# Two output projections in seven block products instead of eight, in a one-core decoder trunk

## The chip, the cores and the metric

The kernel runs on one core of one Trainium2 chip. A core has several engines that run side by side, each with its own queue of instructions in order: TensorE (PE in the profile, with its weight loads as PEld), VectorE (DVE), ScalarE (ACT), GpSimd (POOL) and SyncE (SP), which here only issues transfers. TensorE multiplies a stationary tile of 128x128 by a moving tile of up to 512 columns and adds the result up in PSUM, a memory of eight banks of 128 x 512 fp32; everything else lies in SBUF, which has 128 partitions. The metric is the device time of one execution in microseconds (us); lower is better. An execution is compared with others of the same kernel by the median.

## The reference

Two layers over 1024 rows of 1024 columns in fp32. Each layer runs 12 mixer heads (layer 0: latent attention over all earlier rows; layer 1: attention in a window of 128 rows) and 4 heads over a memory of 256 rows; their outputs of 64 columns each are put side by side, go through one output projection `w_o` of 1024x1024, and are added to the residual. Then follows an MLP. Cut to what matters:

```python
for i in range(DEPTH):                       # DEPTH = 2
    hn = rmsnorm(x, attn_norm_g[i])
    mix, q_cross = mla_mixer(...) if i % 2 == 0 else swa_mixer(...)   # 12 heads x 64
    cross = memory_cross_attention(q_cross, mem_n, w_mem_kv[i])       # 4 heads x 64
    x = x + jnp.concatenate([mix, cross], axis=-1) @ w_o[i]           # the projection
    x = x + squared_relu_mlp(rmsnorm(x, mlp_norm_g[i]), mlp_w_up[i], mlp_w_down[i])
return rmsnorm(x, final_norm_g)
```

## The kernel before

Every fp32 matmul is made of three matmuls of a faster type. `split` (L96) cuts a tile into a high part (a copy on ScalarE, L99) and a low part (a subtraction on VectorE, L100), and `mm3` (L105) adds hi x hi, hi x lo and lo x hi into one PSUM tile (L108 to L110). A product of 128x128 by 128x512 therefore costs three matmuls of 512 columns and, once for each operand, one split.

The program is written as Python that emits instructions. A scheduler orders them at compile time: an instruction is put where its operands and its buffer are ready, in the order of the program where several are, so a load is often issued long ahead of the place where it is written. On the chip each engine then works off its queue in order. Nearly all transfers are issued from SP's queue; the residual's copies into DRAM (`xd`) go by POOL's queue. Tiles are named by tags, and two tiles with one tag share memory: the later one waits for the last reader of the earlier. `quad` holds the large ones (`q0`, `q1`, `f0`, `f1`, and two of `raw`), the `Mlp` object the rest (`i`, `d`, `g`, `x`, `u`).

The work around the projection in each layer:

- *Attention.* The heads' outputs end in two tiles `o[0]` and `o[1]` of 128 x 4 x 1024, features on partitions: together eight k tiles of 128 features by 1024 rows. In layer 0 a head's output is divided by its softmax sum after the fact. For the last head, 11, this is `LastHead` (L1010): the sums go to DRAM, are spread over 64 partitions by another transfer (L1021), and multiplied in (L1028). Its columns lie in k tile 1 of the second half. One of its two halves of rows (G=1) is done at the end of the attention through the list `tails`, the other (G=0) inside the projection.
- *Output projection*, `wo_phase` (L1207): two halves of 512 columns of `w_o`; in each, eight tiles of 128 rows; in each, eight k tiles x 3 matmuls of 128x512: 384 matmuls a layer into tiles `pswo`. Half 0's weights are loaded and split by `WoHalf` (L620) during the attention into `q0` and `q1`; half 1's during half 0 into `g0` to `g3`. For layer 1, `wo_ahead` (L659) makes half 0's split weights some 130 us ahead into DRAM, from where they are loaded again. Each result is added to the residual on VectorE (L1315 in half 0, L1351 in half 1). In half 1 a row tile is then complete: its mean square and its root (L1194 to L1203), the normalised rows (`norm`, L1270) and their transposition (`xT_`, L1278: eight TensorE transposes, L1286, copies by ScalarE, L1289, and for row tiles 4 to 7 four subtractions on VectorE, L1293 to L1296) follow one row tile behind the matmuls; the last row tile's transposition (`m.last_T`) stands in the MLP's first steps.
- *MLP*, `mlp` (L1380). It is already made of seven block products in place of eight. Its operand is cut into two row halves and two column halves; `X[1]` and `X[2]` are the split blocks of rows 0 to 511, written by `xT_`, while `X[3]` to `X[7]` are splits of differences (`prep_x`, L1450). The weight blocks' sums are made by `sum_w` (L1399; L1407 to L1410 are its four operations). The first two of 16 column groups have their products 1 and 2 ahead of the rest, with weights made by `fill_w` (L1370) during the projection; so the order is (0,1), (0,2), (1,1), (1,2), then the other products of these two groups, and then group 2 with its product (2,1) and so on (`go`, L1542; matmuls at L1468 to L1470, results on VectorE at L1499 to L1532).

PSUM is divided in two ways: in the attention of layer 0 six tiles of one bank and one of two (`new_psum(1)`), elsewhere two tiles of two banks (`ps2`) and four of one (`ps1`). The change back stands after `wo_phase(0, ...)`.

Three other places matter for the change. In layer 0, before the attention, `values_of` (L602, tile `psv`) makes the heads' values in eight steps, then six steps make the keys (`pskn`), and then the queries' weights are loaded and split: `wqn` into the pool `wu`, `wqn2` into a pool `wu2` that is opened there; the queries (`psqn`) read them, beside the rotary part (`q_rope`, VectorE). In layer 1, `wo_ahead` runs during the last four jobs of the input projection in two quarters of `f1`, and `s_qk(0, ...)` then writes `f1`. The tiles that `WoHalf.step` fills are filled during the attention, a step every few units.

## Time and profile before

| | |
|---|---|
| runs of the kernel before | 2116.82, 2120.81, 2121.93 us; median 2120.81 |
| the profiled execution | 2116.59 us, of which the span of the trace is 2114.9; granted TensorE clock 0.998 |
| busy share of the span | PE 98%, PEld 81%, DVE 70%, ACT 54%, POOL 8% |
| output projection, layer 0 | first matmul 446.72, end of the last 539.3 us |
| output projection, layer 1 | first matmul 1394.49, end of the last 1487.4 us |
| first product of group 2 of the MLP, (2,1) | 582.43 in layer 0, 1528.64 in layer 1 |

The page of the profile gives shares over the whole span; they are averages over stages with different limits. A row of the timeline gives an instruction's start, its duration, its engine, line and tiles, and in brackets how long the engine had been idle before it and what released it. Matmuls are pipelined: a row's duration (0.39 us) is longer than the distance to the next row. In the chain of waits, a row is a piece of the path that ended last. Lines are those of the kernel before.

### The profile page before, as it was taken

To read this page: it belongs to the slowest core of one execution; us is meant where nothing else is said; L and a number is where in the kernel's file an instruction comes from. 1 tells how busy PE (TensorE), PEld (TensorE's weight loads), DVE (VectorE), ACT (ScalarE), POOL (GpSimd) and SP (SyncE) were. 2 spreads that over 40 slices of the span, in tenths; PEclk is the share of its full clock that TensorE was granted. 3 is DMA by queue.
4 is the path that set the end of the run, shared out by engine and by line. 5 is a ranking of instruction groups with operands and counts; after the bars stand their busy time and mean duration, and the time that the engine had idled before them with its cause. 6 is when DMAs were issued, how large, how long until landed. Compare 5 with 4: busy or idle time off the path is not lost.

```text
span 2114.9 us, 29110 instructions
## 1 busy us (share of the span) xinstructions
PE 2078.4 (98%) x9928; PEld 1708.0 (81%) x9928; DVE 1470.6 (70%) x2833; ACT 1134.6 (54%) x2444; POOL 159.6 (8%) x224
## 2 busy tenths in 40 slices
PE   7999999999999999999999999999999999999998
PEld 6988777788788878888888878778888878788886
DVE  7555588865977776976657553866976775976565
ACT  5455477776754443444445553976745443444452
POOL 0013100001000000000001241620000000000000
PEclk9999999999999999999999999999999999999999
DMA  7202123342354446944433241242344446844342
GB/s 247 68 1 76 46 65 92 105 143 100 110 170 162 140 136 218 337 159 143 150 119 95 66 146 54 81 137 73 133 146 159 157 139 230 317 151 155 118 122 85
DMA packets 177070, 282.92 MB, mean 134 GB/s; under 512 B 17581, under 2 KB 73370, under 8 KB 176922
## 3 DMA queue, kind: packets, MB, share of 16 engines
q1 hardware_dynamic: 170480, 265.30, 39.2%
q0 software_dynamic: 4016, 13.12, 1.8%
q10 hardware_dynamic: 2426, 2.65, 0.4%
q8 instruction: 78, 1.28, 0.3%
q14 instruction: 70, 0.57, 0.1%
HBM read 187.47 MB, written 81.05 MB: 127 GB/s over the span
## 4 chain that ended last, share of the span: by engine, by line
PE 80%; DVE 7%; DMA 6%; ACT 4%; issue 2%; SPq 0%; POOL 0%; DVEq 0%; ACTq 0%; POOLq 0%
PE psy L1805 5%; PE psy L1803 5%; PE psy L1804 5%; PE psz L1805 4%; PE psz L1803 4%; PE psz L1804 4%; PE pss L930 4%; PE pso L972 4%; PE psu L1468 3%; PE psu L1470 3%; PE psu L1469 3%; DMA mr<-in_mlp_w_up_dram 3%; PE pswo L108 3%; PE pswo L110 3%; PE pswo L109 2%; PE psf L108 2%
## 5 line engine op out<-in xcount | busy, mean ns | idle before, releaser
L1368 ACT ACTIVATE mr<-mr,gcol 128x256 f32<-128x256 f32 (+1 forms) x160 | 67.3, 477 | 81.2 <-DMA mr<-in_mlp_w_up_dram 77.5
L1368 ACT ACTIVATE d<-d,gcol 128x256 f32<-128x256 f32 x128 | 57.7, 499 | 79.0 <-DMA d<-in_mlp_w_up_dram 61.7
L1803 PE MATMUL psy<-g 128*128 128x512 f32 x256 | 99.9, 390 | 0.0
L1804 PE MATMUL psy<-g 128*128 128x512 f32 x256 | 99.6, 389 | 0.0
L1805 PE MATMUL psy<-g 128*128 128x512 f32 x256 | 99.4, 389 | 0.0
L99 ACT ACTIVATE g<-i 128x512 fp32r<-128x512 f32 x79 | 49.6, 628 | 89.1 <-PE psz L1804 46.3
L100 DVE TENSOR_TENSOR g<-i,g 128x512 fp32r<-128x512 f32 x79 | 55.5, 703 | 48.9 <-ACT g L99 48.9
L99 ACT ACTIVATE uh<-i 128x512 fp32r<-128x512 f32 x66 | 41.6, 630 | 86.1 <-PE psy L1804 40.7
L99 ACT ACTIVATE i<-mr 128x512 fp32r<-128x512 f32 x78 | 49.1, 629 | 70.8 <-PE psy L1804 20.6
L951 ACT ACTIVATE p<-pss 128x512 f32<-128x512 f32 x108 | 63.6, 593 | 41.1 <-PE pss L930 41.0
L100 DVE TENSOR_TENSOR pl<-p,ph 128x512 fp32r<-128x512 f32 (+1 forms) x96 | 61.5, 651 | 27.4 <-ACT ph L99 26.9
L805 DVE TENSOR_REDUCE m<-psx 128x1 f32<-128x128 f32 (+5 forms) x96 | 70.1, 747 | 11.0 <-PE psx L801 10.8
L100 DVE TENSOR_TENSOR uh<-i,uh 128x512 fp32r<-128x512 f32 x66 | 45.6, 690 | 44.7 <-ACT uh L99 44.7
L1804 PE MATMUL psz<-g 128*128 128x512 f32 x192 | 74.7, 389 | 0.0
L1805 PE MATMUL psz<-g 128*128 128x512 f32 x192 | 74.7, 389 | 0.0
L1803 PE MATMUL psz<-g 128*128 128x512 f32 x192 | 74.7, 389 | 0.0
L100 DVE TENSOR_TENSOR i<-mr,i 128x512 fp32r<-128x512 f32 x78 | 53.6, 687 | 22.0 <-ACT i L99 21.6
L1684 DVE TENSOR_TENSOR mqf<-mqq,mqf 128x512 f32<-128x512 f32 x64 | 43.1, 686 | 21.9 <-DMA mqq<-in_mlp_w_down_dram 21.7
L99 ACT ACTIVATE ph<-p 128x512 fp32r<-128x512 f32 (+1 forms) x96 | 56.4, 599 | 1.3
L1805 PEld LDWEIGHTS psy<-g 128*128 128x128 f32 x256 | 48.1, 188 | 10.0
L1804 PEld LDWEIGHTS psy<-g 128*128 128x128 f32 x256 | 48.1, 188 | 9.9
L1803 PEld LDWEIGHTS psy<-g 128*128 128x128 f32 x256 | 48.1, 188 | 9.8
(658 smaller groups left out, 6913.4 us busy)
## 6 DMA issues: line engine op xcount, KB each, us to landing
i<-hd SPq DMA_DIRECT2D x154, 256.0 KB
hd<-uh SPq DMA_DIRECT2D x76, 256.0 KB
hd<-ul SPq DMA_DIRECT2D x76, 256.0 KB
mr<-in_mlp_w_up_dram SPq DMA_DIRECT2D x36, 512.0 KB
hd<-x SPq DMA_DIRECT2D x72, 256.0 KB
mr<-hd SPq DMA_DIRECT2D x70, 256.0 KB
d<-in_mlp_w_up_dram SPq DMA_DIRECT2D x32, 512.0 KB
mqq<-in_mlp_w_down_dram SPq DMA_DIRECT2D x32, 512.0 KB
```

The costliest lines, as they stand in the source:

```text
L99: nc.scalar.activation(hi, src, AF.Copy)
L100: nc.vector.tensor_tensor(lo, src, f32(hi), ALU.subtract)
L108: nc.tensor.matmul(ps, ah, bh, start=first and i == 0, stop=False)
L110: nc.tensor.matmul(ps, al, bh, start=False, stop=last and i == n - 1)
L805: nc.vector.reduce_max(m8s[h][:, i : i + 1], ps[:, c], axis=AX, negate=True)
L930: return lambda: nc.tensor.matmul(o, a, b, skip_group_check=True, **kw)
L951: nc.scalar.activation(p, ps, AF.Exp, scale=SC)
L972: mms.append(lambda: nc.tensor.matmul(o, a, b, skip_group_check=True, **kw))
L1368: nc.scalar.activation(w[:, k, :], w[:, k, :], AF.Copy, scale=g_mlp[layer][:, k0 + k : k0 + k + 1])
L1803: nc.tensor.matmul(ps, ah[:, j, :], bh, start=p in (1, 5, 2) and k == 0, stop=False, skip_group_check=True)
L1804: nc.tensor.matmul(ps, ah[:, j, :], bl, start=False, stop=False, skip_group_check=True)
L1805: nc.tensor.matmul(ps, al[:, j, :], bh, start=False, stop=k == NP - 1, skip_group_check=True)
```

## The change

The product of activations and `w_o` is cut into 2x2 blocks: rows 0 to 511 and 512 to 1023, k tiles 0 to 3 and 4 to 7, columns 0 to 511 and 512 to 1023. Seven products of such blocks, each of 4 row tiles x 4 k tiles x 3 matmuls of 128x512, replace the eight. Their operands are the blocks themselves or sums of blocks, and their results are added into the output blocks.

- *Weights.* `wo_sums` makes four sums of weight blocks (for products 5, 7, 6 and 4) in eight pieces of 256 columns, splits them and stores the parts to DRAM; a piece has four loads, four subtractions, four splits and eight stores, and all pieces use the same 128 x 6 x 256 tile. In layer 0 it runs beside `values_of` and the keys, in a pool `wop` that is released before `wu2` is opened; in layer 1 in the quarters of `f1`, in the place of `wo_ahead`, with two steps at a time. `WoRaw` replaces `WoHalf`: during the attention it loads the two raw blocks b11 and b22 into `q0` and splits b11 into `q1`.
- *Projection.* `wo_phase` runs 28 steps: products 1, 5, 6, 3, 2, 7, 4, each with k tiles 0, 2, 3, 1. Activation sums (`sums`) are made on VectorE up to seven steps ahead, the splits (`prep`) up to four. Weight sums come back from DRAM in `prep`. Products 1, 6, 7 and 4 add up in the PSUM tiles `pswy`, products 5, 3 and 2 in `pswz`, and at the end of each product four additions put the tiles into the output blocks. Rows 0 to 511 are complete after product 2 and are normalised in place during product 7; rows 512 to 1023 are complete after product 4, whose matmuls run row tile by row tile. Row tiles 0 to 3 are transposed during product 4, tile 4 after it, and tiles 5 to 7 in the MLP between its first products (`m.late`).
- *Last head.* Both halves of head 11 are divided after the first four preparations of the projection (`last_heads`), where PSUM is divided anew, too.

The diff, cut to its core (lines of context and of the removed `WoHalf`, `wo_ahead` and old `wo_phase`, which are shown above, are left out):

```diff
     def split(src, hi, lo, scale=None):

         if scale is None:
-            nc.scalar.activation(hi, src, AF.Copy)
+            r = nc.scalar.activation(hi, src, AF.Copy)
             nc.vector.tensor_tensor(lo, src, f32(hi), ALU.subtract)
+            return r
...
+    def w_rows(layer, k, cols, dst):
+        if layer == 0 or k > 5:
+            nc.sync.dma_start(out=dst, in_=w_o[layer, k * P : k * P + P, cols])
+            return
...
+    wts = {}
+    def wo_sums(layer, buf):
+        ds = wts[layer] = {p: [dram.tile([P, 4, 512], F32, name=f"wt{layer}_{p}{e}") for e in "hl"] for p in (5, 7, 6, 4)}
+        s = [buf[:, i, :] for i in range(6)]
+        V = nc.vector.tensor_tensor
+        def run():
+            for n in range(8):
+                k, c = divmod(n, 2)
+                cs = [slice(e * 512 + c * 256, e * 512 + c * 256 + 256) for e in range(2)]
+                for i, (kt, e) in enumerate(((k, 0), (k, 1), (k + 4, 1), (k + 4, 0))):
+                    w_rows(layer, kt, cs[e], s[i])
+                yield
+                V(s[0], s[1], s[0], ALU.subtract)
+                V(s[1], s[2], s[1], ALU.subtract)
+                V(s[2], s[2], s[0], ALU.subtract)
+                V(s[3], s[3], s[2], ALU.subtract)
+                for i, p in enumerate((5, 7, 6, 4)):
+                    hi, lo = s[4 + i % 2].bitcast(F32R), s[i].bitcast(F32R)
+                    split(s[i], hi, lo)
+                    for d_, t_ in zip(ds[p], (hi, lo)):
+                        nc.sync.dma_start(out=d_[:, k, c * 256 : c * 256 + 256], in_=f32(t_))
+                    if i % 2:
+                        yield
+        return run()
+    class WoRaw:
+        def __init__(self, layer):
+            self.layer, self.n = layer, 0
+        def step(self):
+            n, k = self.n, self.n % 4
+            self.n += 1
+            if n == 0:
+                self.q = quad_tile("q0", f"wor{self.layer}")
+            if n == 4:
+                self.q1 = quad_tile("q1", f"wob{self.layer}", F32R)
+            if n < 4:
+                w_rows(self.layer, k, slice(0, 512), self.raw(0, k))
+                w_rows(self.layer, k + 4, slice(512, 1024), self.raw(1, k))
+            elif n < 8:
+                split(self.raw(0, k), *self.b1(k))
+        def raw(self, e, k):
+            return self.q[:, k, e * 512 : e * 512 + 512]
+        def b1(self, k):
+            return [self.q1[:, k, e * 512 : e * 512 + 512] for e in range(2)]
+    wop = pool("wop", "right")
+    summing = wo_sums(0, wop.tile([P, 6, 256], F32, name="wos"))
...
         values_of(t)
+        for _ in range(2):
+            next(summing, None)
-    class WoHalf:
...
-    def wo_ahead(buf):
...
+        for _ in range(2):
+            next(summing, None)
         nc.vector.tensor_copy(kn[j][:, 0:512], ps[:, 0:512])
         nc.scalar.activation(kn[j][:, 512:1024], ps[:, 512:1024], AF.Copy)
+    wop.release()
     wu2 = pool("wu2", "right")
     wqn = rows(wpair(wu, 2, 768, "wqn", "a"), 2) + rows(wpair(wu2, 1, 768, "wqn2", "c"), 1)
...
-    wq = WoHalf(0, 0, quad_slots())
+    wq = WoRaw(0)
...
-        if n == len(seq) + LB - 2:
-            tails[0].spread(at.tile([P, 512], F32, tag="p", bufs=4, name="rb11"))
     for _ in muls:
         pass
-    tails[0].mul()
...
-    def wo_phase(layer, wq, o, m):
...
+    def wo_phase(layer, wo, o, m, head=None):
+        ADD, V = ALU.add, nc.vector.tensor_tensor
+        X, xr = {}, {}
+        m.X, m.xr, m.t2, m.fill = X, xr, {}, []
+        steps = [(p, k) for p in (1, 5, 6, 3, 2, 7, 4) for k in (0, 2, 3, 1)]
+        N = len(steps)
+        a1 = [m.t(f"i{2 * j}")[:, 0, :] for j in range(4)]
+        u2 = [m.t(f"i{2 * j + 1}")[:, 0, :] for j in range(4)]
+        a5 = [v_[:, j, :] for v_ in (m.t("d2"), m.t("d3")) for j in range(2)]
+        c21 = []
+        def load(dst, r, c):
+            for j in range(4):
+                nc.sync.dma_start(out=dst[j], in_=m.x_src[r * 512 + j * P : r * 512 + j * P + P, c * 512 : c * 512 + 512])
+        load(a1, 0, 0)
+        load(a5, 1, 1)
+        load(u2, 0, 1)
+        def A(k, e, r):
+            return o[e][:, k, r * 512 : r * 512 + 512]
+        s_ = [v_[:, j, :] for v_ in (m.t("uh"), m.t("ul")) for j in range(2)]
+        ga = [m.t(f"g{i}", F32R) for i in range(4)]
+        gb = [m.t(f"x{i}", F32R) for i in (1, 3, 0, 2)]
+        slots = [[[g_[i // 2][:, 2 * (i % 2) + e, :] for e in range(2)] for g_ in (ga, gb)] for i in range(8)]
+        def sums(n):
+            p, k = steps[n]
+            if p == 5:
+                V(s_[k], A(k, 0, 1), A(k, 1, 1), ADD)
+            if p == 6:
+                V(s_[k], s_[k], A(k, 0, 0), SUB)
+            if p == 3:
+                V(s_[k], A(k, 1, 0), s_[k], SUB)
+            if p == 7:
+                V(A(k, 0, 1), A(k, 0, 0), A(k, 0, 1), SUB)
+        ops, his, b21 = {}, [], []
+        def prep(n):
+            p, k = steps[n]
+            a = s_[k] if p in (5, 6, 3) else A(k, *{1: (0, 0), 2: (1, 0), 7: (0, 1), 4: (1, 1)}[p])
+            (ah, al), (bh, bl) = slots[n % 8]
+            his.append(split(a, ah, al))
+            if p == 1:
+                bh, bl = wo.b1(k)
+            elif p in (3, 2):
+                split(wo.raw(1, k) if p == 3 else b21[0][:, k, :], bh, bl)
+            else:
+                for t_, d_ in zip((bh, bl), wts[layer][p]):
+                    nc.sync.dma_start(out=f32(t_), in_=d_[:, k, :])
+            ops[n] = (k4(ah), k4(al), bh, bl)
+        for n in range(4):
+            prep(n)
+        if head:
+            with tc.issue_after(his[1].ins):
+                head()
+        Y = [ps2(f"pswy{layer}_{i}") for i in range(2)]
+        Y = [Y[j // 2][:, (j % 2) * 512 : (j % 2) * 512 + 512] for j in range(4)]
+        Z = [ps1(f"pswz{layer}_{j}") for j in range(4)]
+        res = {1: (Y, a1), 5: (Z, a5), 6: (Y, u2), 3: (Z, u2), 2: (Z, a1), 7: (Y, a5), 4: (Y, c21)}
+        def mm(n, j):
+            p, k = steps[n]
+            ah, al, bh, bl = ops[n]
+            ps = res[p][0][j]
+            first, last = n % 4 == 0, n % 4 == 3
+            nc.tensor.matmul(ps, ah[:, j, :], bh, start=p in (1, 5, 2) and first, stop=False, skip_group_check=True)
+            nc.tensor.matmul(ps, ah[:, j, :], bl, start=False, stop=False, skip_group_check=True)
+            nc.tensor.matmul(ps, al[:, j, :], bh, start=False, stop=last, skip_group_check=True)
+        def add(p, j):
+            ps, dst = res[p]
+            nc.vector.tensor_tensor(dst[j], ps[j], dst[j], ADD)
+        ys, rst = {}, {}
+        def ends(t):
+            return (a1[t], u2[t]) if t < 4 else (c21[t - 4], a5[t - 4])
+        def junk(t, i):
+            if t not in ys:
+                ys[t] = m.t(f"d{4 + t % 2}")
+            return ys[t][:, i, :]
+        def stat(t, i):
+            if t not in rst:
+                rst[t] = Rstd()
+            x_ = ends(t)[i]
+            nc.gpsimd.dma_start(out=xd[t * P : t * P + P, i * 512 : i * 512 + 512], in_=x_)
+            rst[t].half(1 - i, x_, junk(t, i))
+        def norm(t):
             rs = rst.pop(t).get()
+            xs = ends(t)
+            y = ys[t] = xs if t < 4 else [junk(t, i) for i in range(2)]
+            nc.scalar.activation(y[0], xs[0], AF.Copy, scale=rs)
+            nc.vector.tensor_scalar(y[1], xs[1], rs, None, ALU.mult)
+        def xT_(t):
+            y = ys.pop(t)
             j, late_col = t % 4, t >= 4
             c = slice(j * P, (j + 1) * P)
...
+                n = 2 * i + late_col
+                if n not in xr:
+                    xr[n] = m.t(f"x{n}")
+                nc.scalar.activation(xr[n][:, :, c], k4(ps), AF.Copy)
             if late_col:
                 r = [xr[i][:, :, c] for i in range(4)]
                 m.t2[j] = t2 = k4(m.t(f"i{2 * j}")[:, 0, :])
                 nc.vector.tensor_tensor(r[0], r[1], r[0], SUB)
                 nc.vector.tensor_tensor(t2, r[3], r[0], SUB)
+                V(r[1], r[3], r[1], SUB)
+                V(r[2], r[2], t2, SUB)
+        nsum, nprep = 0, 4
+        for n in range(N - 4):
+            while nsum < min(N, n + 7):
+                sums(nsum)
+                nsum += 1
+            while nprep < min(N, n + 5):
+                prep(nprep)
+                nprep += 1
+            if n == 4:
+                b21.append(m.quad("q1"))
+                for k in range(4):
+                    w_rows(layer, k + 4, slice(0, 512), b21[0][:, k, :])
+            if n == 12:
+                c21 += [m.t(i)[:, 0, :] for i in ("i31", "i32", "i39", "i30")]
+                load(c21, 1, 0)
+            if n in (16, 18):
+                m.fill.append(fill_w(layer, m, n // 2 - 8))
+            for j in range(4):
+                mm(n, j)
+            p = steps[n][0]
+            if n % 4 == 3:
+                for j in range(4):
+                    add(p, j)
+                    if p == 3:
+                        stat(j, 1)
+                    elif p == 2:
+                        stat(j, 0)
+                    elif p == 7:
+                        stat(4 + j, 1)
+            if p == 7:
+                norm(n % 4)
+        for i in range(2):
+            q = m.quad(f"q{i}", F32R)
+            X[i + 1] = [q[:, 0:4, :], q[:, 4:8, :]]
+        for j in range(4):
+            for n in range(N - 4, N):
+                mm(n, j)
+            add(4, j)
+            stat(4 + j, 0)
+            if j < 3:
+                xT_(j)
+            if j == 2:
+                xT_(3)
+            norm(4 + j)
+        xT_(4)
+        m.late = [lambda t=t: xT_(t) for t in (5, 6, 7)]
...
         open_x()
         load_raw(0)
+        m.late[0]()
         go(0, 1, m.fill[0][1])
-        m.last_T()
+        m.late[1]()
         go(0, 2, m.fill[0][2])
+        m.late[2]()
         gain_w(0)
         sum_w(0)
         prep_x(6, range(3))
...
-    wo_phase(0, wq, [f0, f1], m0)
-    new_psum(2)
+    def last_heads():
+        lb = [raw_tile([P, S], f"lastb{i}") for i in range(2)]
+        heads = [LastHead(1, lb[0][0:65, 512:1024], lb[1][:, 0:32]), LastHead(0, m0.t("i32")[0:65, 0, :], m0.t("i31")[:, 0, 0:32])]
+        new_psum(2)
+        for f, rb in zip(heads, (lb[0][:, 0:512], m0.t("i39")[:, 0, :])):
+            f.spread(rb)
+        for f in heads:
+            f.mul()
+    wo_phase(0, wq, [f0, f1], m0, last_heads)
...
             if n == 3 and not i:
-                wods, ahead = wo_ahead(f1[:, 0:2, :])
-            if n > 2:
-                next(ahead, None)
+                summing = wo_sums(1, f1[:, 0:2, :].rearrange("p a (b c) -> p (a b) c", c=256))
+            for _ in range(2 if n > 2 else 0):
+                next(summing, None)
...
-    wq = WoHalf(1, 0, quad_slots(), wods)
+    wq = WoRaw(1)
```

195 lines of the change are left out of this document (5 added, 190 removed).

## The prediction, on record before the result

> **What bounds the kernel now.** I read the page's shares and its chain of waits first, then the windows of the stages that the change touches, then single rows. Of the page:
>
> ```profile
> span 2114.9 us, 29110 instructions
> PE 2078.4 (98%) x9928; PEld 1708.0 (81%) x9928; DVE 1470.6 (70%) x2833; ACT 1134.6 (54%) x2444; POOL 159.6 (8%) x224
> PE 80%; DVE 7%; DMA 6%; ACT 4%; issue 2%; SPq 0%; POOL 0%; DVEq 0%; ACTq 0%; POOLq 0%
> ```
>
> TensorE is busy for 98% of the span, so a matmul left out should pay its full price, unless the work that stood beside it becomes the wait. That is asked stage by stage. A row of the windows gives the stretch, its length, and each engine's busy time with its instructions, then the granted clock:
>
> ```profile
> 446.72:490.30 43.58, 43.58 (x194) 36.07 (x194) 25.46 (x40) 29.32 (x66) 3.85 (x7) 1.00 0.59 191
> 490.30:539.30 49.00, 49.00 (x241) 40.83 (x239) 34.72 (x83) 32.39 (x70) 4.32 (x8) 1.00 0.26 87
> 539.30:582.40 43.10, 40.73 (x185) 33.08 (x184) 40.57 (x73) 32.81 (x68) 0.54 (x1) 1.00 0.30 104
> 1487.40:1528.60 41.20, 40.70 (x185) 32.94 (x185) 38.75 (x70) 33.21 (x70) 0.54 (x1) 1.00 0.35 118
> 157.00:203.00 46.00, 44.60 (x280) 36.56 (x279) 25.18 (x48) 27.88 (x85) 13.26 (x7) 1.00 0.23 61
> 203.00:217.00 14.00, 13.95 (x88) 13.22 (x86) 13.24 (x40) 6.72 (x21) 8.97 (x14) 1.00 0.41 114
> 1222.00:1312.00 90.00, 89.32 (x445) 72.69 (x445) 46.17 (x61) 40.20 (x76) 26.49 (x43) 1.00 0.36 117
> 1340.00:1394.00 54.00, 53.61 (x384) 38.01 (x380) 44.18 (x187) 48.76 (x175) 37.11 (x42) 1.00 0.01 2
> ```
>
> The first two rows are layer 0's output projection: TensorE never idles. The third, the start of the MLP, is of another kind: VectorE is busy 40.57 of 43.10 us and TensorE idles 2.4. The chain of waits there:
>
> ```profile
> 546.90 0.60 DVE d L1407
> 547.50 0.60 DVE g L100
> 548.10 0.60 DVE x L1293
> ...
> 581.78 0.61 DVE x L1512
> 582.43 0.50 PE psu L1468
> ```
>
> From 542.42 to 582.43 it is almost all VectorE, one 512-wide operation per 0.60 us. At 582.43 the first product of the MLP's third step begins; it waits for VectorE. So each projection is bound by TensorE, and the 40 us behind it by VectorE. Layer 1's stage (1487.40 on) has the same form with less idle time.
>
> **The matmuls removed.** On TensorE, with start, duration and line:
>
> ```profile
> 523.84 0.39 PE L108 MATMUL pswo<-g,d 128*128 128x512 f32 x1
> ...
> 532.67 0.40 PE L110 MATMUL pswo<-g,d 128*128 128x512 f32 x1
> 532.90 1.03 PE L1286 MATMUL psT_m<-ident,d 128*128 128x128 f32 x8
> 533.69 0.48 PE L108 MATMUL pswo<-g,d 128*128 128x512 f32 x1
> ...
> 539.04 0.39 PE L110 MATMUL pswo<-g,d 128*128 128x512 f32 x1
> 540.42 1.09 PE L1286 MATMUL psT_m<-ident,d 128*128 128x128 f32 x8 [1.00 <-ACT d L1275]
> 542.44 0.50 PE L1468 MATMUL psu<-mqq,uh 128*128 128x512 f32 x1 [0.92 <-ACT x L1289]
> ```
>
> From 523.84 to 532.67 are 39 steps: 0.2265 us each. Eight products of blocks (2 column halves x 8 row tiles x 8 k x 3 = 384 matmuls) become seven (7 x 4 k x 4 x 3 = 336), so 48 go in each layer: 96 x 0.2265 = **-21.7**. The Trainium skill ("TensorE: Matmul & The Clock Gate", section "Back-to-back issue gap") gives about 131 ns a matmul of 512 columns as the sustained gap; by it the 96 would be worth 12.6 us. No row here is near it, and the measured gap stands.
>
> **VectorE inside the projection.** By groups, with count, busy time, mean ns and the idle time before:
>
> ```profile
> L1351 DVE TENSOR_TENSOR i<-pswo,i 128x512 f32<-128x512 f32 x8 | 5.5, 690 | 6.0 <-PE pswo L110 5.9
> L1315 DVE TENSOR_TENSOR i<-pswo,i 128x512 f32<-128x512 f32 x8 | 5.4, 686 | 6.3 <-PE pswo L110 6.2
> L1276 DVE TENSOR_SCALAR d<-i,cosb 128x512 f32<-128x512 f32 x4 | 1.9, 484 | 0.1
> ```
>
> New there: 16 additions of PSUM become 28, and 16 sums of activations appear; the splits are 28 of activations and 8 of weights. That is 80 operations x 0.60 = 48 us; with the rows' statistics (some 6), seven norms (0.5 each) and the splits of the first four transposed tiles (8 x 0.60) 62, beside 336 x 0.2265 + 4 x 0.8 = 79.3 us of matmuls and four transposed tiles. It is covered. Weight sums come back by 32 loads (256 KB each, 8 MB); with the x tiles and raw blocks some 18 MB in 80 us, where the first window moved 191 GB/s, 15 MB a stage: tight at the start, covered on average.
>
> But consecutive products use the same banks: 3 then 2 on Z, 7 then 4 on Y. Four additions stand at each border, and the next product's first matmul on a bank waits for its addition. The first is free 0.7 us after the last matmul and the others follow at 0.6, while a bank's turn comes each 3 x 0.2265 = 0.68 us. Between nothing and 1 us a border (an addition queued behind a split, 0.6): four borders, **+2** [0 to +4].
>
> **The ends of the projection.** Before, the row tiles end one at a time, and only the last is transposed after the last matmul. Now rows 4 to 7 all need product 4, the last. Behind its end come, on VectorE, the transposed sums of three or four tiles (four subtractions each, L1293 to L1296; of tiles 4 and 5 in full, 8 x 0.60 = 4.8), one more norm (0.5), and the combinations that read them (some five operations, 3.0), in each layer 8.3 us, up to 10.7 with one of the MLP's weight sums. They meet the stage whose chain is VectorE: 40.57 + 8.3 = 48.9 us of work where TensorE has 38.1 + 3 x 0.8 = 41. What excuses some is VectorE's idle time there (2.5 us) and inside the projection (14.3 us in the second window, but what could fill it waits for buffers that the products hold). Bounds for a layer: 0, if the scheduler finds enough of the fill's work to do early; +9, if none. Before had 14.3 us idle in the same place and did not fill it, so I take the middle: **+10** for both [0 to +18].
>
> **The starts.**
>
> ```profile
> 445.91 0.68 DVE L1058 TENSOR_TENSOR fa<-rb,fa 64x512 f32<-64x512 f32 x1
> 454.95 0.69 DVE L1029 TENSOR_TENSOR fa<-rb,fa 64x512 f32<-64x512 f32 x1 [4.15 <-DMA rb<-rcl]
> 1394.49 0.50 PE L108 MATMUL pswo<-woq,d 128*128 128x512 f32 x1 [0.88 <-ACT d L99]
> ```
>
> Layer 0: product 1 reads half 0 and the first 512 rows, so it needs no last head. The two last heads (before, one of them ran in the attention) now take the DMA round trip that here ended at 454.95 after 4.15 us; they are needed by product 5's last step, 1.75 products or some 19 us after the start. But its slots lie on memory that the last multiplication (445.91) reads, and its four splits stand in front: **+1** [0 to +3]. Layer 1: raw block and split wait ready in q0 and q1, so the 0.88 us goes: **-0.9** [-1 to +1]. Its four splits of weights, 4 x 0.52 on ScalarE, move into a stage where it is busy 48.76 of 54: **+0.5** [0 to +2].
>
> **The weight sums, layer 0.** Eight pieces, each four loads (128x256), four subtractions, four splits, eight stores on SP's queue, and one buffer, which the next piece waits for. The nearest rows are the weights made ahead for layer 1:
>
> ```profile
> 1260.02 0.32 SPq L676 DMA_DIRECT2D wodl<-fb  x1
> 1262.88 0.33 SPq L667 DMA_DIRECT2D fb<-in_w_o_dram  x1
> 1265.65 0.63 ACT L99 ACTIVATE fb<-fb 128x512 fp32r<-128x512 f32 x1 [2.23 <-DMA fb<-in_w_o_dram]
> ```
>
> The next load goes out 2.86 us after the store that it waits for, and ScalarE starts 2.77 after the load. Half the bytes may take 2.2. A piece: load 2.5, subtractions 4 x 0.35, two splits 0.8, a store (two slots serve four splits) 2.5, two splits 0.8, a store 2.5 = 10.5; 8.4 where the next loads overlap the last stores. Eight: 67 to 84 us. It begins with the values:
>
> ```profile
> L117 PE MATMUL psv<-wkvh,ckh x32: 333/335/445, 140.9 to 182.1; 128*128 128x384 f32 x32
> 218.39 0.39 PE L108 MATMUL psqn<-cTh,wqn2h 128*128 128x512 f32 x1
> ```
>
> From 140 to 146 on, it ends at 207 to 230. wqn2 takes the same memory and is read at 218.39, behind a load (2.8) and its splits (1.2): the stall is the end + 4 - 218.4. The 64 operations of VectorE (22 us) have room until 203 (25.18 busy of 46), none from 203 to 217 (13.24 of 14), where its ropes feed TensorE. Queued behind a waiting load on SP are the loads of the later weights. Ends: 0, and 230 + 4 - 218 = 16; from the middle of the spread, 218: **+4** [0 to +16].
>
> **The weight sums, layer 1.** The same work from job 3 on, with 64-row loads, inside a stage with VectorE at 46.17 of 90; it replaces 16 splits made there. I expect it to end about when f1 is wanted, 1312: **+1** [0 to +5].
>
> The skill ("SBUF — State Buffer", section "Who interferes with whom") holds that a VectorE instruction with two SBUF inputs contends with a GpSimd instruction that reads SBUF; that is the fourth rival, priced there from rows.
>
> **Sum.** -21.7 + 1 + 4 + 10 + 2 - 0.9 + 1 + 0.5 = -4.1. The profiled execution took 2116.59 (span 2114.9 and 1.7 around it), so 2112.5 in its terms. The median of the runs, 2120.81, lies 4.2 higher; against it **2116.7**.
>
> **The rivals.** First, *the covers hold*: VectorE's extra work at the ends finds the 14.3 us of idle time, and the sums end before 212. Then only start, banks and half a tail stay: -21.7 + 5 = -16.7, or **2104**. For it speaks TensorE's 98%; against it a stage at 94% on VectorE. Second, the other side, *late sums gate wqn2*: the chain of pieces ends at 230, and 16 us stand in place of 4: -4.1 + 12 = +8, **2129**. It decides from an end at about 222, where the stall is 8 and no gain is left; from 229 on it is a loss that can be measured. For it: three DMA round trips in a piece; against it: the scheduler may start it before 140. Third, *the banks and slots serialise the products*: four borders at 2 us, not 0.5: +6 more, **2123**. Fourth, *VectorE and GpSimd block each other*. Rows:
>
> ```profile
> 1258.97 1.01 DVE L100 TENSOR_TENSOR fb<-fb 128x512 fp32r<-128x512 f32 x1 [1.46 <-ACT fb L99]
> 1266.32 1.59 DVE L100 TENSOR_TENSOR fb<-fb 128x512 fp32r<-128x512 f32 x1 [1.37 <-ACT fb L99]
> ```
>
> The 512-wide operations above take 0.69; these, with POOL busy 26.49 of 90, 0.3 and 0.9 more. With 0.3 more on each of the sums' 64 operations in layer 0, where POOL is busy 13.26 of 46 and 8.97 of 14, the chain ends some 10 us later, of which about 5 reach the path: **2122**. The rule in the skill agrees with these two rows; subtractions of matmul results are free of it.
>
> **How the numbers follow.** Forecast 0.44 (own range 2110 to 2123), covers hold 0.30, late sums 0.15, borders 0.05, blocked VectorE 0.06. A change under 0.3% (6.4 us) can't be told from none here. Faster: all of the first rival and a quarter of the forecast, 0.42. Slower by over 6.4: most of the late sums, and the far ends of the rest, 0.19; the rest, 0.39, is within. The range goes from the first rival's better half, 2102, to the late sums, 2129.
>
> **What would show it.** 9832 matmuls and transposes instead of 9928; psu's third step 135.7 - 10.9 + 6 us after the projection's start (446.72 to 582.43 before). The wait of psqn on wqn2 at 218 shows the late sums; VectorE saturated behind product 4 with TensorE waiting on L1293 to L1296 and on the combinations shows the tail; waits on pswz and pswy at the borders the banks. I am wrong if TensorE's idle time behind the projections stays as it was: then the gain is some 10 us larger.

## The result, and the profile after

The changed kernel takes 2177.83 us (median of 5, 2176.25 to 2178.65), the kernel before 2120.26: a ratio of 1.0272, 95% interval 1.0257 to 1.0287. It is 57 us slower; the forecast was 2116.7. (One of the ten executions of the kernel `start` below took 11819.96 us and is left out of its median and its ratio.) Of the page of the changed kernel:

```profile
span 2176.1 us, 29775 instructions
PE 2080.5 (96%) x9832; PEld 1700.2 (78%) x9832; DVE 1556.4 (72%) x3013; ACT 1149.4 (53%) x2504; POOL 161.5 (7%) x224
PE 60%; DMA 13%; DVE 9%; ACT 5%; issue 2%; SPq 1%; POOL 0%; DVEq 0%; ACTq 0%
```

The 96 matmuls are gone (9928 to 9832). TensorE's share of the chain fell from 80% to 60%, that of transfers rose from 6% to 13%, and TensorE's busy time did not fall at all: some matmuls run longer, as the last section shows. Whom TensorE waits for (in total, times, longest):

```profile
PE psqt L842 <- POOL fa L304: 20.8, 1, 20.8
PE psw L2004 <- DVE fb L2009: 12.3, 1, 12.3
...
PE pswz L1258 <- DVE i L1264: 3.9, 1, 3.9
...
PE pswy L1258 <- ACT fa L1002: 2.5, 1, 2.5
...
PE pswy L1260 <- DVE g L100: 2.1, 1, 2.1
```

The two longest stand far from the projections: the transposition of the rotary queries in layer 0, and layer 1's first scores. Both are places where the weight sums were put. To see the whole, I cut the spans at the same points of the program, all by the start of a matmul: the first of the values (`psv`), of the queries (`psqn`) and of each projection, the last of the attention (`pso`) and of each projection, and the first of the 20th product of the MLP behind it.

| stage, us | before | after | no sums | arithmetic only | transfers only |
|---|---|---|---|---|---|
| values to queries, layer 0 | 76.0 | 111.2 | 76.0 | 91.7 | 83.1 |
| queries to end of attention | 229.7 | 228.9 | 228.7 | 228.9 | 229.0 |
| from there to the projection | 0.1 | 2.8 | 2.8 | 2.9 | 2.9 |
| projection, layer 0 | 92.3 | 90.9 | 89.8 | 88.0 | 92.1 |
| its end to product 20 | 57.1 | 66.5 | 63.6 | 62.3 | 64.6 |
| MLP and layer 1 up to its projection | 798.3 | 822.0 | 801.4 | 804.8 | 801.0 |
| projection, layer 1 | 92.7 | 81.7 | 82.0 | 81.6 | 81.8 |
| its end to product 20 | 55.1 | 62.8 | 67.1 | 64.8 | 64.9 |
| before the first, after the last | 713.5 | 709.3 | 707.3 | 711.3 | 709.2 |

(The last three columns are the experiments nosum, deadops and deaddma below. Each column is one profiled execution; those of nosum and deadops, 2120.41 and 2138.01 us, were the fastest of their kernels, both 4.6 below the median.) After less before: 35.2 in layer 0's values and queries, 23.7 up to layer 1's projection, 9.4 and 7.7 behind the projections, 2.7 at the first one's start, and gains of 0.8 in the attention, 1.4 and 11.0 in the projections and 4.2 elsewhere: 61.3 us between these two spans, 57 between the medians. Layer 1's projection gains 11.0, about what 48 matmuls cost, but that is two things that happen to cancel: two of its six transposed tiles (16 transposes, some 1.6 us) now stand behind its end as well, and it waits 1.4 us for a weight sum to come back from DRAM (`x<-wt_5h`, at 1473.6).

The first stage in windows, before and after:

```profile
140.90:216.90 76.00, 73.74 (x463) 64.26 (x461) 50.56 (x119) 46.16 (x141) 26.36 (x26) 1.00 0.21 58
```
```profile
138.70:249.90 111.20, 79.77 (x462) 68.44 (x461) 80.67 (x182) 57.64 (x172) 26.19 (x26) 0.86 0.50 153
```

VectorE's work rises from 50.56 to 80.67 us, more than the 76 us that the stage took. Of these 30.1 us some 6.5 come from five of the sums' 64 operations that ran beside one of GpSimd's, and took 1.2 to 2.1 us where the others took 0.42; for instance:

```profile
170.54 2.11 POOL L428 TENSOR_TENSOR cps<-cps,cst 128x1024 f32<-128x1024 f32 x1 [1.14 <-DVE cst L426]
```
```profile
170.93 2.00 DVE L627 TENSOR_TENSOR wos<-wos 128x256 f32<-128x256 f32 x1
```

The second operation of the rotary part before, and then the stage's end in the changed kernel, by tile (first and last start) and in order of time:

```profile
204.66 0.34 DVE L299 TENSOR_TENSOR ra<-psqr,sinb 128x192 f32<-128x192 f32 x1
```

```profile
L603 SPq DMA_DIRECT2D wos<-in_w_o_dram x32: 328/402/1564, 144.2 to 224.7; - x32
...
L633 SPq DMA_DIRECT2D wt_4l<-wos x8: 333/394/1204, 153.5 to 233.3; - x8
```
```profile
235.58 0.36 DVE L300 TENSOR_TENSOR ra<-psqr,sinb 128x192 f32<-128x192 f32 x1 [2.72 <-DMA qk1l<-kl]
```
```profile
236.01 0.59 POOL L303 TENSOR_TENSOR fa<-fa,ra 128x192 f32<-128x192 f32 x1 [45.09 <-DVE ra L300]
```

The eight pieces run from 144.2 to the last store's issue at 233.3, 11.1 us each. The rotary part's second operation starts only behind that, at 235.58: 96.9 us after the values' first matmul, where it was 63.8 before. These 33.1 us are nearly all of the stage's 35.2.

Behind the projection of layer 0 (from its end to product 20), before and after:

```profile
539.10:596.20 57.10, 54.70 (x247) 44.42 (x246) 52.97 (x93) 40.73 (x86) 0.54 (x1) 1.00 0.39 135
```
```profile
572.70:639.00 66.30, 61.52 (x262) 48.51 (x261) 59.32 (x107) 44.27 (x94) 0.54 (x1) 0.92 0.34 112
```

VectorE has 14 instructions and 6.4 us more to do there, and the clock granted to TensorE falls to 0.92.

### The profile page after: what moved, and what is told of

Its sections match the earlier page's. It is cut to its first block, busy times and chain, and to the rows that moved or that the text cites. A ratio compares the mean times of both kernels' runs of the same rounds, so it can differ in the third digit from the quotient of the medians.

```text
span 2176.1 us, 29775 instructions
## 1 busy us (share of the span) xinstructions
PE 2080.5 (96%) x9832; PEld 1700.2 (78%) x9832; DVE 1556.4 (72%) x3013; ACT 1149.4 (53%) x2504; POOL 161.5 (7%) x224
## 4 chain that ended last, share of the span: by engine, by line
PE 60%; DMA 13%; DVE 9%; ACT 5%; issue 2%; SPq 1%; POOL 0%; DVEq 0%; ACTq 0%
PE psy L1799 5%; PE psy L1801 5%; PE psy L1800 5%; DMA mr<-in_mlp_w_up_dram 4%; PE psz L1799 4%; PE psz L1800 4%; PE psz L1801 4%; PE pss L917 4%; PE pso L959 3%; DMA d<-in_mlp_w_up_dram 3%; PE psu L1462 3%; PE psu L1463 3%; PE psu L1464 3%; PE psv L1464 1%; PE psv L1463 1%
## 5 line engine op out<-in xcount | busy, mean ns | idle before, releaser
L938 ACT ACTIVATE p<-pss 128x512 f32<-128x512 f32 x108 | 63.6, 593 | 43.5 <-PE pss L917 43.4
L789 DVE TENSOR_REDUCE m<-psx 128x1 f32<-128x128 f32 (+5 forms) x96 | 70.3, 749 | 11.1 <-PE psx L785 10.8
L1801 PEld LDWEIGHTS psy<-g 128*128 128x128 f32 x256 | 48.0, 188 | 10.1
```

The lines of the kernel that those rows point to most:

```text
L789: nc.vector.reduce_max(m8s[h][:, i : i + 1], ps[:, c], axis=AX, negate=True)
L1801: nc.tensor.matmul(ps, al[:, j, :], bh, start=False, stop=k == NP - 1, skip_group_check=True)
```

## The experiments

Ratios are to the kernel before on the same chip, 4 to 10 executions each, with the 95% interval. The kernel before has medians from 2115.56 to 2118.40 there, so kernels are compared by their ratios.

| kernel | median, us | ratio |
|---|---|---|
| nosum | 2125.03 | 1.0039 (1.0024 to 1.0053) |
| order0 | 2173.76 | 1.0268 (1.0253 to 1.0284) |
| slots1 | 2170.17 | 1.0249 (1.0234 to 1.0264) |
| attn0 | 2176.20 | 1.0275 (1.0256 to 1.0294) |
| pool0 | 2210.35 | 1.0430 (1.0414 to 1.0446) |
| deadops | 2142.58 | 1.0108 (1.0093 to 1.0123) |
| swap | 2126.21 | 1.0030 (1.0018 to 1.0042) |
| notsub | 2106.30 | 0.9936 (0.9920 to 0.9953) |
| deaddma | 2130.17 | 1.0069 (1.0054 to 1.0084) |
| start | 2117.59 | 1.0006 (0.9996 to 1.0015) |
| pooltail | 2127.20 | 1.0054 (1.0039 to 1.0069) |
| mended | 2160.83 | 1.0221 (1.0203 to 1.0240) |
| noload | 2149.26 | 1.0145 (1.0127 to 1.0163) |
| nostore | 2148.69 | 1.0148 (1.0129 to 1.0168) |
| slots01 | 2158.73 | 1.0186 (1.0164 to 1.0208) |
| mended2 | 2155.70 | 1.0176 (1.0161 to 1.0191) |

**Is it the sums at all?** nosum:

```diff
-    summing = wo_sums(0, wop.tile([P, 6, 256], F32, name="wos"))
+    summing = iter(())
...
...
-                for t_, d_ in zip((bh, bl), wts[layer][p]):
+                for t_, d_ in zip((bh, bl), wts[layer] if layer in (0, 1) else wts[layer][p]):
```

Here `wts[layer]` is the stored split of b11.

> The changed kernel with no weight sums made in either layer: products 5, 6, 7 and 4 take the split of block b11 from DRAM instead (stored once in each attention, eight stores of 256 KB a layer), so their loads stay as many and as large; left out are the sums, so the output is not the product. Theory 'sums' (nearly all of the loss of 57 us comes from making the sums ahead): the 33 us by which layer 0's queries come late and the 13.5 us at layer 1's first scores go, with some of the 8 us lost around the latter: 2125, between 2119 and 2132. Rival 'projection' (the new order inside the projection and behind it is what costs): less than half goes, above 2150.

2125, as theory 'sums' had it: by the ratios 0.0233 of 0.0272, some 49 of the 57 us, belong to the sums. It also says that the change without its sums is not faster either: 1.0039, some 8 us slower.

**What of the sums, layer 0.** order0 changes which tiles lie on the memory of `wos`:

```diff
     wu2 = pool("wu2", "right")
+    for g_, sh_, b_ in (("ra", [P, H, 16], 2), ("rb", [P, H, 16], 2), ("wraw", [P, 4, 96], 1)):
+        wu2.tile(sh_, F32, tag=g_, bufs=b_, name=f"first_{g_}")
```

> The changed kernel with the tiles of pool wu2 laid out in another order, so that the rotary temporaries ra and rb and the raw weights lie beside the sums' tile wos, and only wqn2 on it. Nothing is left out. Theory 'memory' (what waits is whoever is next on the memory of wos, until the last store has landed at 235.5): the rotary part runs at its old time, and the next reader is wqn2, read at 218.4 before, behind its splits: a stall of some 17 to 21 us in place of 33, so 2177.8 - 14 = 2164, between 2160 and 2168. Rival 'queues' (the sums' waiting instructions in the queues of VectorE, ScalarE and SP hold the rotary part): no change, 2175 to 2181.

The stage took 109.3 in place of 111.2, and slots1 below, whose layer 0 is that of the changed kernel, took 109.6: nothing came back that can be told from none. Its VectorE shows why:

```profile
235.24 0.85 DVE L100 TENSOR_TENSOR wos<-wos 128x256 fp32r<-128x256 f32 x2
236.01 0.35 DVE L300 TENSOR_TENSOR ra<-psqr,sinb 128x192 f32<-128x192 f32 x1
```

The same operation of the rotary part starts at 236.01 without any wait of its own, right behind the sums' last subtraction; the 2.72 us that it waited in the changed kernel, after that subtraction, are gone. So the memory was in its way too, but the order of VectorE's queue holds it just as long. Theory 'memory' falls for layer 0.

attn0 and pool0 move the sums into the attention (in the two raw tiles), the second with the arithmetic and the transfers on GpSimd:

```diff
+    sr = [raw_tile([P, 4, 256], f"wos{i}") for i in range(2)]
+    summing = wo_sums(0, None, [t_[:, i, :] for t_ in sr for i in range(4)])
...
+        if n >= 4 and n % 3 == 1:
+            next(summing, None)
```

> The changed kernel with layer 0's sums made during layer 0's attention instead of beside the values and keys, in the two raw tiles, which the attention does not use (eight slots); a step every third unit. Nothing is left out. Theory 'memory': nothing waits for that memory before the projection, so the whole 33 us goes: 2145, with up to 5 us for 64 more operations (27 us) on VectorE in a stage where it is busy 78%: 2143 to 2151. Rival 'queues': the waiting loads and stores hold the attention's own work on VectorE and SP, and more than half of the gain is given back: above 2161.

> Layer 0's sums in the attention as in attn0 (same tiles, same pieces, same loads and stores), but all their arithmetic on GpSimd, which is idle there, and their transfers in GpSimd's own queue. Nothing is left out; layer 1 is as in the changed kernel. Theory 'queues' (a piece is a chain of DMA round trips, and its waiting instructions stand in the queues of SP and VectorE ahead of other work's): with both queues free of them the 33 us of layer 0 go, 2144, between 2138 and 2152. Rival 'transfers' (what is late is late because of the sums' bytes and their time on the DMA engines): as much as attn0, above 2165.

Both designs had a fault: the raw tiles hold `qr2` and `krs`, parts of queries and keys that the attention reads until its last head is loaded, so the sums began at 387.7 and were squeezed in ahead of the projection.

```profile
PE pss L911 <- DMA qh<-mh: 17.8, 1, 17.8
```
```profile
POOL wos L611 <- DMA q<-qr: 142.0, 1, 142.0
```

In attn0 the values' stage is back at 76.0, and the attention takes 262.7 in place of 228.9: the loss moved with the sums almost whole. What waits now is the load of a head's row maxima, which stands in SP's queue among the sums' transfers (first row, attn0). In pool0 the attention loses 12, and the projection then waits 34.6 and 29.9 us. So neither tells queues from transfers; attn0 shows that the loss goes where the sums go.

**Arithmetic or transfers.** Into nosum, one half of the sums at a time is put back:

```diff
 (deadops, noload)
+                    if n == 0:
                         w_rows(layer, kt, cs[e], s[i])
 (deadops, nostore)
-                    for d_, t_ in zip(ds[p], (hi, lo)):
-                        nc.sync.dma_start(out=d_[:, k, c * 256 : c * 256 + 256], in_=f32(t_))
 (deaddma: no V(...), no split)
+                    for d_ in ds[p]:
+                        nc.sync.dma_start(out=d_[:, k, c * 256 : c * 256 + 256], in_=s[i])
```

> The kernel without sums (its products 5, 6, 7 and 4 take the split of block b11, as in nosum), with the sums' arithmetic alone put back in both layers at its places: 64 operations on VectorE and 32 on ScalarE a layer on the first piece's data, without the other pieces' loads and without any store. Left out are so the loads, the stores and the sums as operands. Theory 'queues': without round trips the arithmetic waits for nothing and fits into VectorE's idle time: 2125 + 0 to 8, between 2125 and 2134. Rival 'work' (27 us more on VectorE a layer in stages where it is on the path): above 2145.

> The kernel without sums (as nosum) with the sums' transfers alone put back in both layers at their places and in their buffers: every load, and two stores of each loaded block, without any arithmetic. Left out are so the sums as operands. Theory 'both' (in layer 0 it is VectorE's 64 operations, some 16 us by deadops, and their waits for the round trips; in layer 1 the time at which f1 comes free): layer 0 loses 0 to 3 us, layer 1, whose pieces are now about 12 us long, 5 to 12 as in slots1: 2126 + 10, between 2130 and 2142. Rival 'SP' (the weights' loads of layer 0 stand behind the sums' transfers in SP's queue): layer 0 alone loses some 15: above 2146.

> The kernel without sums (as nosum) with the sums' arithmetic and stores in both layers, but the loads of the first piece only; left out are the other loads and the sums as operands. Arithmetic alone cost 15 us (deadops), transfers alone 6 (deaddma), all together 52. Theory 'stores' (the waits that make the rest are those for a store to land before its slot is written again): most of the rest stays, 2160 to 2172. Theory 'loads' (VectorE's first subtraction of a piece waits for its load with other work behind it): 2141 to 2150. Theory 'chain' (only a whole round of load, arithmetic and stores in one buffer is long enough to come late): between them in both this kernel and nostore, 2145 to 2158.

> The same with all loads and without any store; left out are the stores and the sums as operands. Theory 'stores': 2141 to 2150. Theory 'loads': 2160 to 2172. Theory 'chain': 2145 to 2158, as noload.

Against nosum (76.0 and 801.4), by stage (the four other kernels without sums below, swap, start, notsub and pooltail, have 76.0 to 76.1 and 800.7 to 803.7, so some 3 us in the second column tell nothing):

| put back | values to queries | up to layer 1's projection |
|---|---|---|
| arithmetic | +15.7 | +3.4 |
| transfers | +7.1 | -0.4 |
| arithmetic and stores | +19.9 | +6.3 |
| arithmetic and loads | +14.2 | +13.3 |
| all (the changed kernel) | +35.2 | +20.6 |

deadops lies between its two theories. deaddma lies in the range of theory 'both', at its lower edge, but only by its sum: that theory put 0 to 3 us into layer 0 and 5 to 12 into layer 1, and the stages show 7.1 and nothing. noload (2149.26) lies in the ranges of 'loads' and 'chain', nostore (2148.69) in those of 'stores' and 'chain'; 'stores' and 'loads' each ask for one of the two above 2160, so 'chain' alone fits both. In layer 0 the arithmetic alone costs nearly half:

```profile
139.90:231.60 91.70, 79.18 (x463) 67.05 (x461) 81.81 (x184) 57.50 (x173) 27.27 (x27) 0.94 0.18 52
```

VectorE is busy 81.81 of 91.70: a stage that had been TensorE's is now VectorE's. Of the rest, 7 us come with the transfers alone and, if these two add up, 12 only with load, arithmetic and stores together. In layer 1 neither arithmetic nor transfers alone cost much, arithmetic with loads 13.3, and all of it together 20.6. Whether the length of a piece's round is the cause, slots1 and slots01 ask:

```diff
-        s = [buf[:, i, :] for i in range(6)]
+        s = [buf[:, i, :] for i in range(buf.shape[1])]
+        nh = len(s) - 4
...
-                    hi, lo = s[4 + i % 2].bitcast(F32R), s[i].bitcast(F32R)
+                    hi, lo = s[4 + i % nh].bitcast(F32R), s[i].bitcast(F32R)
...
 (slots01 as well)
-    summing = wo_sums(0, wop.tile([P, 6, 256], F32, name="wos"))
+    summing = wo_sums(0, wop.tile([P, 8, 256], F32, name="wos"))
```

> The changed kernel with eight slots instead of six for layer 1's sums (two quarters of f1 have room for eight), so that each of a piece's four splits has a slot of its own and need not wait for an earlier store. Nothing is left out; layer 0 is as it was. Theory 'latency' (layer 1 loses because eight pieces, each a chain of DMA round trips in one buffer, end at 1376 where f1 is wanted at about 1361): a piece is some 2.5 us shorter, the chain ends about 20 us earlier, and the wait of 12.3 us with the slow matmuls behind it goes: 2177.8 - 13 = 2165, between 2162 and 2169. Rival 'queues' (as many instructions, as many bytes): 2174 to 2180.

> The changed kernel, nothing left out, with eight slots instead of six for the sums in both layers (slots1 had them in layer 1). Theory 'chain': layer 0's pieces get some 2 us shorter, its chain ends 16 us earlier and so does what waits for it: 2177 - 6 - 14, between 2150 and 2163. Rival (VectorE's work alone sets layer 0's loss): no more than slots1, 2166 or more.

Layer 1's stores of one kind (first and last start) and the wait that follows in the changed kernel, then these stores in slots1, and layer 0's in slots01:

```profile
L633 SPq DMA_DIRECT2D wt_4l<-fb x8: 320/382/537, 1280.1 to 1376.0; - x8
```
```profile
1377.84 0.47 PE L2004 MATMUL psw<-kh,q 128*128 128x128 f32 x1 [12.30 <-DVE fb L2009]
```
```profile
L634 SPq DMA_DIRECT2D wt_4l<-fb x8: 319/392/1324, 1277.6 to 1357.7; - x8
```
```profile
L634 SPq DMA_DIRECT2D wt_4l<-wos x8: 393/399/447, 155.0 to 230.4; - x8
```

In layer 1 a piece takes 11.4 us in place of 13.7 (seven pieces between these stores), close to the 2.5 that theory 'latency' took off; the chain ends 18 us earlier, and the stage gives 10.1 of its 20.6 us back. So there the length of the round is a cause, of half. But TensorE still waits 9.1 us at the first scores, in place of 12.3, where that theory had the wait gone; the ratio fell by 0.0023, some 5 us of the 13 expected, and 2170.17 lies between the two theories. In layer 0, slots01's pieces take 10.8 in place of 11.4 (153.5 to 233.3 before), not 2 us less, and the stage 105.7 in place of 111.2, where 14 us were expected. slots01's median, 2158.73, and its ratio, 0.0063 under slots1's, do fit theory 'chain'; but its executions run from 2155.55 to 2165.57, and the profiled one is the slowest. So the two slots do not set the round in layer 0; what does is open. What the chain waits for in layer 1 (changed kernel, 1247 to 1380):

```profile
DVE fb L625 <- DMA fb<-in_w_o_dram: 17.1, 7, 4.8
...
SPq L633 <- ACT fb L99: 34.4, 20, 7.0
```

VectorE stood 17.1 us before the first subtraction of a piece for its load, with layer 1's own splits and copies behind it in the queue, and SP's queue 34.4 us for ScalarE's copies.

**The start.** swap exchanges the banks of Y and Z; start gives `rb` a second buffer as well, both in nosum:

```diff
+        Z = [ps1(f"pswz{layer}_{j}") for j in range(4)]
         Y = [ps2(f"pswy{layer}_{i}") for i in range(2)]
...
-                rb = at.tile([P, 512], F32, tag="rb", bufs=1, ...
+                rb = at.tile([P, 512], F32, tag="rb", bufs=2, ...
```

> The kernel without sums (as nosum) with the PSUM of the projection the other way round: the four single banks of Z are taken first, so that Y, which product 1 writes, lies in banks 4 to 7 and not on the banks 1 and 3 that the last head's results leave last. Theory 'banks' (the first product waits 2.5 us for ScalarE's copies out of those banks, then 2.2 for a split on VectorE, and some 20 matmuls run at half rate behind it): the first wait goes and with it part of the slow matmuls, 2120 to 2123. Rival: the wait for VectorE's split only gets longer and nothing is gained: 2124 to 2127.

> The kernel without sums with the PSUM the other way round (as swap) and two buffers instead of one for rb, the tile in which the softmax sums of the heads before the last are spread. Left out are the sums only. Theory 'queue' (the split of product 1 stands on VectorE behind a multiplication that waits 3.6 us for the second load of rb): both waits at the start go, and some of the slow matmuls: 2126 - 7, between 2115 and 2121. Rival (the next thing is as late: the loads of product 5 or ScalarE): 2123 or more.

swap won nothing: the first wait (2.5) went, the second grew from 2.2 to 5.2. The reason, in nosum:

```profile
445.82 0.68 DVE L1044 TENSOR_TENSOR fa<-rb,fa 64x512 f32<-64x512 f32 x1 [3.59 <-DMA rb<-rcd]
...
447.64 2.48 DVE L100 TENSOR_TENSOR g<-qn,g 128x512 fp32r<-128x512 f32 x4
```

The split that product 1 needs stands on VectorE behind a multiplication for an earlier head that waits 3.59 us for its load. With two buffers the gap at the start (2.8) and 2.8 us inside the projection go, as theory 'queue' had it, and the ratio is 1.0006, that of the kernel before within its interval.

**The tail.** notsub leaves three of four subtractions per transposed tile out; pooltail puts two of four on GpSimd:

```diff
 (notsub)
-                nc.vector.tensor_tensor(r[0], r[1], r[0], SUB)
...
-                V(r[1], r[3], r[1], SUB)
-                V(r[2], r[2], t2, SUB)
 (pooltail)
+                nc.gpsimd.tensor_tensor(r[1], r[3], r[1], SUB)
+                nc.gpsimd.tensor_tensor(r[2], r[2], t2, SUB)
```

> The kernel without sums (as nosum) with one subtraction instead of four for each of the transposed row tiles 4 to 7; left out are so 12 operations of 0.6 us on VectorE a layer, behind the last product, and the MLP's operands are not the right ones. Theory 'tail' (behind the projection VectorE sets the pace, and TensorE waits for it in places of 1 to 2 us, each with slow matmuls behind it): 7.2 us a layer less, and part of the slow matmuls: 2125 - 14, between 2107 and 2116. Rival (the waits there are for weights or for ScalarE's splits): 2120 or more.

> The kernel without sums with two of the four subtractions of each transposed row tile 4 to 7 on GpSimd, which is idle there; left out are the sums only. Theory 'tail' (VectorE sets the pace behind the projection; notsub won 19 us for 12 operations a layer): 8 operations a layer less on VectorE: 2126 - 11, between 2110 and 2120. Rival (GpSimd takes over 1.4 us for each, and the blocks X7 and X4 or VectorE itself come late): 2123 or more.

The stage behind layer 0's projection, nosum and notsub:

```profile
535.20:598.60 63.40, 59.03 (x261) 46.80 (x260) 59.22 (x107) 43.82 (x93) 0.54 (x1) 0.97 0.35 117
```
```profile
537.90:593.80 55.90, 55.85 (x262) 46.10 (x261) 51.70 (x94) 44.72 (x97) 0.54 (x1) 1.00 0.38 132
```

7.5 us less on VectorE make the stage 7.5 us shorter, and TensorE is then busy throughout. By the ratios notsub wins 0.0103, some 22 us, in place of the 14 expected. So VectorE sets the pace behind the projections. It is not the tail's price, though: the kernel before makes these subtractions too, and the price is the 9.4 and 7.7 of the table. In layer 1 notsub's stage is 10.9 shorter than nosum's, but part of that is nosum's slow matmuls; with as much work on VectorE the changed kernel had none there. The stage behind layer 1's projection, nosum and the changed kernel (the last number but two is the granted clock):

```profile
1482.00:1549.10 67.10, 61.65 (x262) 48.64 (x261) 59.50 (x107) 44.38 (x95) 0.54 (x1) 0.92 0.33 110
```
```profile
1542.70:1605.50 62.80, 57.87 (x262) 45.61 (x261) 59.52 (x107) 44.27 (x94) 0.54 (x1) 1.00 0.36 118
```

On GpSimd the work is not free, and pooltail gained nothing. GpSimd and VectorE in pooltail, then VectorE in the changed kernel:

```profile
544.36 1.46 POOL L1313 TENSOR_TENSOR x<-x,i 128x512 f32<-128x512 f32 x1 [0.76 <-DVE i L1311]
```
```profile
L1311 DVE TENSOR_TENSOR i<-x,x 128x512 f32<-128x512 f32 x4 | 4.6, 1141 | 0.0
L1310 DVE TENSOR_TENSOR x<-x,x 128x512 f32<-128x512 f32 x4 | 3.8, 954 | 0.0
...
L100 DVE TENSOR_TENSOR mqf<-x,mqf 128x512 fp32r<-128x512 f32 x4 | 3.8, 946 | 0.0
```
```profile
L1307 DVE TENSOR_TENSOR x<-x,x 128x512 f32<-128x512 f32 x4 | 2.7, 685 | 0.0
```

The first two subtractions and these splits on VectorE take 0.95 to 1.14 us on average in place of 0.68, and GpSimd's own 1.27 to 1.70: with eight instructions fewer VectorE is busy longer (62.8 us in that stage, against 59.2 in nosum). The rule of the Trainium skill ("SBUF — State Buffer", "Who interferes with whom") that a VectorE instruction with two SBUF inputs contends with a GpSimd instruction that reads SBUF agrees with these rows.

**All together.** mended has slots1, order0, start and pooltail in the changed kernel; mended2 has slots01, order0 and start.

> The changed kernel, nothing left out, with all that is mended so far: eight slots for layer 1's sums, the rotary temporaries beside the sums' tile, the PSUM the other way round, two buffers for rb, and two of four subtractions on GpSimd. If the gains add: 2177 - 6 - 2 - 7 - 11 = 2151, between 2143 and 2158, still above the kernel before by what layer 0's sums cost. Rival (the places of the gains overlap, what is early at one waits at the next): 2162 or more.

> The changed kernel, nothing left out, with eight slots in both layers, the rotary temporaries beside the sums' tile, the PSUM the other way round and two buffers for rb (mended without the work on GpSimd, and with eight slots in layer 0 too). If the gains add: 2177 - 6 - 14 - 2 - 7 = 2148, between 2140 and 2156. Rival (they overlap): 2160 or more.

mended, 2160.83, lies between its two theories, and mended2, 2155.70, at the upper edge of the one in which the gains add: they overlap in part. order0 and start, which is worth 7 us in the kernel without sums, take the ratio of slots01 from 1.0186 only to 1.0176. Nothing that computes the whole came under the kernel before. Layer 0's stage is still 103.7 in mended2 (76.0 before), and layer 1's 812.4 (798.3).

## Why the prediction was wrong

- *The matmuls*: the price is right, 10.9 a layer. That layer 1's projection measured 11.0 is partly luck: two tiles' transposes (1.6) moved out of it, and a wait of 1.4 for a weight sum came in.
- *Weight sums, layer 0*: the step that failed, in the overlap. +4 (0 to +16) stands against 35.2. The chain itself was sized nearly right: 10.5 us a piece forecast, 11.1 measured, end at 207 to 230 forecast, some 235.5 measured. Wrong was the sentence that the 64 operations "have room until 203": they were not done by then, but stood in VectorE's queue until 232.4 and held what came behind them. They were priced at 22 us, and VectorE's work rose by 30.1; the arithmetic alone cost 15.7 (deadops). Wrong, too, was to price one reader of one memory, wqn2 at 218: wqn2's first part was written at 232.30, ahead of the sums' last store, so it did not wait for that memory. What waited was the rotary part, due at 204.66, behind the sums in VectorE's queue, and the queries come only behind it: from its second operation to the first query product it took 12.3 us before and 14.4 after. The forecast's formula, the end + 4 - 218.4, gives 21 even with the measured end.
- *Weight sums, layer 1*: "I expect it to end about when f1 is wanted": +1 forecast, 20.6 measured. I had not worked out its piece. It takes 13.7 us, with loads of 64 rows and stores that wait for a ScalarE that is busy with other work, and the first one 33 (first load at 1247.0, last store at 1280.1): half of its loads wait 10.2 us for TensorE's transpositions (`psvT`) to read the memory that they write.
- *The ends*: mechanism right, size off. +5 a layer (0 to +9) stands against 9.4 and 7.7, together at the top of the range; notsub shows that VectorE sets the pace there. I left out that TensorE's stalls there slow the matmuls behind them.
- *The starts*: +1 forecast, 5.6 by start. The last multiplication and the four splits ahead of product 1 were seen; that its PSUM banks come late (2.5 us), and that the splits stand behind a multiplication which itself waits 3.59 us for a load, was not. The -0.9 in layer 1 did not come (0.88 us of waiting before, 0.88 after).
- *Banks*: +2 forecast. In layer 1 no wait at a border shows, and 81.7 us are 2.4 above the 79.3 worked out, 1.4 of them for the weight sum; layer 0 shows one wait of 3.9 at the border from product 3 to 2.
- *Rivals*: "late sums gate wqn2" had late sums right and the reader wrong, with 0.15. Its price for layer 0, 16 us, is under half of the 35.2 that came, and it left layer 1 as it was. "VectorE and GpSimd block each other" is seen, but on five of the 64 operations and not on each; what these 6.5 us cost on the path no run tells.

## What to carry to other kernels

Work that is made ahead is not priced by an engine's idle share alone: loads, arithmetic and stores in one buffer make a chain, and what is queued behind its instructions can come as late as the chain does. Before moving work to an engine with idle time, add it up against the stage's length, and look what chain of that engine the bound engine already waits for. A saving of 48 matmuls is real only where the engine next in line has that much time to spare: here 17.1 us behind the two products and 2.7 ahead of the first took back nearly all of the 21.7.

## What the hardware showed that was not expected

Behind short stalls TensorE ran at half rate for some microseconds. In the changed kernel, behind layer 0's projection, in order of time and then the window around the slow rows, with a granted clock of 0.50:

```profile
588.19 0.49 PE L1462 MATMUL psv<-mqf,d 128*128 128x512 f32 x1 [0.63 <-ACT mqf L99]
...
591.73 0.80 PE L1463 MATMUL psu<-mqf,i 128*128 128x512 f32 x1 [1.25 <-DVE mqf L100]
592.32 0.63 PE L1464 MATMUL psu<-mqf,i 128*128 128x512 f32 x1
...
594.88 0.63 PE L1464 MATMUL psu<-mqf,i 128*128 128x512 f32 x1
```
```profile
590.50:597.30 6.80, 5.49 (x12) 3.80 (x12) 6.80 (x12) 3.21 (x7) 0.00 (x0) 0.50 0.10 39
```

From 592.32 to 594.88 six steps take 2.56 us, 0.427 each in place of 0.2265, though no single wait was longer than 1.25 us; three waits of 0.63, 0.54 and 1.25 came within 4 us. The Trainium skill ("TensorE: Matmul & The Clock Gate", "Back-to-back issue gap") gives N / 1.2 ns for a cold array, 427 ns for 512 columns: the rows agree. So these stalls cost more than their length. How much idle time it takes these rows do not tell: in the kernel before, waits of 1.00 and 0.92 us stand within 3 us at the same place (540.42 and 542.44), and the granted clock there is 1.00.
